# Loads and stores of a 1-D max pooling kernel, issued from GpSimd as one packet per DMA engine

## The chip, the cores and the metric

The kernel runs on one core of a Trainium2 chip. A core has five instruction queues: TensorE, VectorE, ScalarE, GpSimd and SyncE (SP); all but the first matter here. Its 16 DMA engines move data between the chip's memory (DRAM) and the on-chip buffer of 128 partitions. The metric is the device time of one execution in microseconds, the median of several runs. The profile is one further execution.

## What is computed

The input is float32 with 32 x 256 rows of 4096 values; the output has 256 values per row, each the largest of 16 neighbours.

```python
def reference(x: np.ndarray, output_size: int) -> np.ndarray:
    batch, channels, length = x.shape
    result = np.zeros((batch, channels, output_size), dtype=np.float32)
    for i in range(output_size):
        start = int(i * length / output_size)
        end = int((i + 1) * length / output_size)
        result[:, :, i] = np.max(x[:, :, start:end], axis=-1)
    return result
```

The input is 134.22 MB and the output 8.39 MB; 4096 / 256 = 16 without remainder, so every window has the same width W = 16.

## The kernel before

The 2,097,152 windows lie one behind the other in memory. They are dealt out in two groups, each cut evenly over the 128 partitions: group A has 9340 windows per partition, group B 7044. Within a group a partition's share is contiguous, so one row of a load is one contiguous stretch of memory.

**Loads.** Group A is read in ten loads (one of 128 windows per partition, eight of 1024, one of 1020), from the end of the share to its start; group B in seven (six of 1024, one of 900), from start to end. A load of 1024 windows is 128 rows of 65,536 bytes. The first, small one (line 87) goes to the space between the two slots' ends and serves to give VectorE work early; all others come from line 96.

**The ring.** The tile `ring` holds two slots of 1024 + 152 windows. A load uses one slot, and which 1024 of the 1176 windows it uses alternates: loads 0 and 1 lie at the low end of their slots, loads 2 and 3 are moved up by 152 (GAP), and so on. So the next load into a slot leaves 152 windows of the load before it untouched.

**Reductions.** `pooled` (line 56) is one VectorE reduction over the last axis. Each large load is reduced in two instructions: first the 872 windows that the next load into this slot will overwrite, then the 152 that it will not. The results go to the tile `kept` (the last load's to a part of the ring that has become free). The load after next can therefore be issued once the 872 are done, while the 152 are still being reduced.

**Stores.** Two large stores (line 117) write group A's and most of group B's results from `kept`. They stand behind all loads on SP's queue. The first needs nothing that is still to come when the last load has been issued; the second waits for the last reduction into `kept`. The last 900 windows per partition are stored by ScalarE (line 114), as soon as the last reduction ends.

**Order.** The framework derives the semaphores from the tiles. In the program, SP's queue holds the first load, two loads without waits, fourteen loads that each wait for a VectorE reduction (and for the landing of the load whose place they take), and the two stores. GpSimd's queue has four MEMSETs of constants at the start, which belong to the launch (line 134), and the barriers at the start and the end of the program. VectorE's queue holds only the reductions. All engines pass a barrier at the start and one at the end.

Of the kernel before, what the change touches and what calls it, by code (L numbers as in the profile page):

```python
# [1 line left out]

# [4 lines left out]


@with_exitstack
def kernel(  # L10
    ctx: ExitStack,
    tc: tile.TileContext,
    x: bass.AP,
    output_size: bass.AP,
    out: bass.AP,
):

    nc = tc.nc
    P = nc.NUM_PARTITIONS
    fp32 = mybir.dt.float32

    B, C, L = x.shape
    O = int(output_size)  # L30
    assert L % O == 0, (L, O)
    W = L // O
    total = B * C * O // P
    assert B * C * O % P == 0

    CHUNK = 1024
    GAP = 152
    FIRST = 128
    LOADS_A, LOADS_B = 9, 6

    LESS = 4
    group_a = [FIRST] + [CHUNK] * (LOADS_A - 1) + [CHUNK - LESS]
    last = total - sum(group_a) - LOADS_B * CHUNK
    group_b = [CHUNK] * LOADS_B + [last]
    assert 0 < last and last * (W + 1) <= CHUNK * W

    pool = ctx.enter_context(tc.tile_pool(name="pool", bufs=1))
    ring = pool.tile([P, 2 * (CHUNK + GAP) * W], fp32, tag="ring", name="ring")
    kept = pool.tile([P, total - last], fp32, tag="kept", name="kept")

    xw = x.flatten_outer_dims().rearrange("r (o w) -> (r o) w", w=W)
    ow = out.flatten_outer_dims().rearrange("r o -> (r o)")

    def pooled(dst, at, n):

        nc.vector.reduce_max(  # L56
            out=dst,
            in_=ring[:, at * W : (at + n) * W].rearrange("p (n w) -> p n w", w=W),
            axis=mybir.AxisListType.X,
        )  # L60

    taken = 0

    def group(n):

        nonlocal taken
        span = slice(taken * P, (taken + n) * P)
        taken += n
        return (
            xw[span].rearrange("(p n) w -> p (n w)", p=P),  # L70
            ow[span].rearrange("(p n) -> p n", p=P),
        )

    stores = []
    n_loads = 0
    base = 0
    for g, loads in enumerate((group_a, group_b)):
        xg, og = group(sum(loads))
        a = sum(loads) if g == 0 else 0
        for n in loads:  # L80
            if g == 0:
                a -= n
            xn = xg[:, a * W : (a + n) * W]
            dst = kept[:, base + a : base + a + n] if n != last else None
            if n == FIRST:

                nc.sync.dma_start(  # L87
                    out=ring[:, CHUNK * W : (CHUNK + n) * W], in_=xn
                )
                pooled(dst, CHUNK, n)  # L90
            else:

                low = n_loads % 2 * (CHUNK + GAP)
                moved = n_loads // 2 % 2
                at = low + moved * GAP
                nc.sync.dma_start(out=ring[:, at * W : (at + n) * W], in_=xn)
                if n != last:
                    cut = CHUNK - GAP if moved else GAP
                    parts = [(0, cut), (cut, n)]
                    for u, v in parts if moved else parts[::-1]:  # L100
                        pooled(dst[:, u:v], at + u, v - u)
                else:
                    end = (at + CHUNK) * W
                    last_kept = ring[:, end - n : end]
                    pooled(last_kept, at, n)
                n_loads += 1
            if g:
                a += n
        full = a - last if g else sum(loads)
        stores.append((og[:, 0:full], kept[:, base : base + full]))  # L110
        base += full
    assert taken == total

    nc.scalar.dma_start(out=og[:, full : full + last], in_=last_kept)
    tc.no_sync_barrier()
    for dst, src in stores:
        nc.sync.dma_start(out=dst, in_=src)


# [1 line left out]
_INS = ['x', 'output_size']  # L121
_OUTS = [((32, 256, 256), 'float32')]

_NUMBERS = {'output_size': 256}


# [26 lines left out]
```

## Time and profile before

| | |
|---|---|
| median of 3 runs | 334.98 us (334.91 to 335.12) |
| profiled execution's own span | 333.1 us |
| large loads: number, KB each, us from issue to landing (median) | 14 of the same size at 24.0 us; 8160 KB at 23.9; 7200 KB at 21.7 |
| first load | 1024 KB, 4.7 us |
| stores from SP | 4670 KB, 32.4 us; 3072 KB, 18.2 us |
| store from ScalarE | 450 KB, 4.2 us |
| reduction of 872 windows | 14 times, mean 14,686 ns |
| reduction of 152 windows | 15 times, mean 2,676 ns |
| reduction of the last 900 | 15,143 ns |
| length of a DMA instruction on SP's queue | 327 to 426 ns |
| memory read / written | 134.22 MB / 8.39 MB, 428 GB/s over the span |

The times of runs are taken without the profiler and include what lies around the profiled span. "Issue to landing" runs from the DMA instruction on its queue to the semaphore that says that all its data are there; a transfer that is queued behind another one has the other's remaining time in it. In the views by window the columns are: the stretch and its length, busy time of VectorE and of GpSimd with the number of instructions, the clock granted to TensorE (not used here), the mean share of time in which the 16 DMA engines had a packet, and the rate. A packet is booked whole where its record falls, so shares over 1 and rates that jump appear in stretches shorter than the packets of the loads; only longer stretches, or stretches with short packets, can be read as shares. Transfers are listed by queue: q1 is SP's, q10 is ScalarE's.

### The profile page before, as it was taken

The page shows a single profiled execution, that of the slowest core. Times are in us where ns is not written, and L with a number is a line of the kernel's source. Part 1 is how long each engine was busy: PE and PEld are TensorE (multiplying, and loading weights), DVE is VectorE, ACT ScalarE, POOL GpSimd, SP SyncE. Part 2 cuts the span into 40 slices and gives each one's busy share as a digit, 9 for nine tenths or more (in the row PEclk, how much of TensorE's full clock was granted, in tenths as well). Part 3 has the DMA queues.
Part 4 walks back from the last instruction along what each step waited for, and adds up shares of the span by engine and source line. Part 5 has one row for each costly group of instructions (what it writes and reads, how often), then busy time and mean ns, then how long its engine had stood idle before and what let it go on. Part 6 is the DMA issues. An engine that isn't in the chain of part 4 may idle for free.

```text
span 333.1 us, 113 instructions
## 1 busy us (share of the span) xinstructions
DVE 276.5 (83%) x32; POOL 0.2 (0%) x4
## 2 busy tenths in 40 slices
DVE  2009979797997979799797979979797998979993
POOL 0000000000000000000000000000000000000000
DMA  9898989899898989899898989899898989899997
GB/s 378 378 504 378 504 378 504 378 449 433 378 504 378 504 378 504 378 441 441 384 494 377 504 378 504 378 456 425 386 496 378 504 378 504 378 458 443 393 395 330
DMA packets 2880, 142.61 MB, mean 428 GB/s; under 512 B 320, under 2 KB 320, under 8 KB 448
## 3 DMA queue, kind: packets, MB, share of 16 engines
q1 hardware_dynamic: 2736, 142.15, 98.8%
q10 hardware_dynamic: 144, 0.46, 0.3%
HBM read 134.22 MB, written 8.39 MB: 428 GB/s over the span
## 4 chain that ended last, share of the span: by engine, by line
DMA 57%; DVE 36%; DVEq 5%; issue 0%; SPq 0%
DMA ring<-in_x_dram 57%; DVE kept L56 36%; DVEq L148 5%; SPq L87 0%
## 5 line engine op out<-in xcount | busy, mean ns | idle before, releaser
L56 DVE TENSOR_REDUCE kept<-ring 128x152 f32<-128x2432 f32 (+3 forms) x31 | 261.4, 8473 | 51.5 <-DMA ring<-in_x_dram 51.5
L56 DVE TENSOR_REDUCE ring<-ring 128x900 f32<-128x14400 f32 x1 | 15.1, 15143 | 0.0
L134 POOL MEMSET const-bfloat16-1.0<- 128x1 bf16 x1 | 0.1, 103 | 0.0
L134 POOL MEMSET const-uint8-127<- 128x1 uint8 x1 | 0.1, 102 | 0.0
L134 POOL MEMSET const-float32-0.0<- 128x1 f32 x1 | 0.1, 100 | 0.2 <-issue 0.2
L134 POOL MEMSET const-float32-1.0<- 128x1 f32 x1 | 0.1, 99 | 0.0
## 6 DMA issues: line engine op xcount, KB each, us to landing
ring<-in_x_dram SPq DMA_DIRECT2D x1, 8160.0 KB, 23.9
ring<-in_x_dram SPq DMA_DIRECT2D x1, 7200.0 KB, 21.7
out_dram<-kept SPq DMA_DIRECT2D x1, 4670.0 KB, 32.4
out_dram<-kept SPq DMA_DIRECT2D x1, 3072.0 KB, 18.2
ring<-in_x_dram SPq DMA_DIRECT2D x1, 1024.0 KB, 4.7
out_dram<-ring ACTq DMA_DIRECT2D x1, 450.0 KB, 4.2
ring<-in_x_dram SPq DMA_DIRECT2D x14, 24.0
```

The source lines that it names most:

```text
L56: nc.vector.reduce_max(out=dst, in_=ring[:, at * W : (at + n) * W].rearrange("p (n w) -> p n w", w=W), axis=mybir.AxisListType.X,)
L134: nc = _bacc.Bacc("TRN2", target_bir_lowering=False, num_devices=1)
L148: with _tile.TileContext(nc) as tc:
```

## The change

In three places `nc.sync.dma_start` becomes `nc.gpsimd.dma_start` with `single_packet=True`: the first load, the other sixteen loads, and the two large stores. Sizes, addresses, order and the waits of the transfers stay as they are: GpSimd's queue now has the nineteen DMA instructions between the start's and the end's barrier, and SP's has none. The flag asks that all that one DMA engine moves for one transfer is put into one packet. ScalarE's store stays as it is. The reductions are the same instructions in the same order, and wait for the same transfers.

```diff
@@ -84,8 +84,8 @@
             dst = kept[:, base + a : base + a + n] if n != last else None
             if n == FIRST:
 
-                nc.sync.dma_start(
-                    out=ring[:, CHUNK * W : (CHUNK + n) * W], in_=xn
+                nc.gpsimd.dma_start(
+                    out=ring[:, CHUNK * W : (CHUNK + n) * W], in_=xn, single_packet=True
                 )
                 pooled(dst, CHUNK, n)
             else:
@@ -93,7 +93,9 @@
                 low = n_loads % 2 * (CHUNK + GAP)
                 moved = n_loads // 2 % 2
                 at = low + moved * GAP
-                nc.sync.dma_start(out=ring[:, at * W : (at + n) * W], in_=xn)
+                nc.gpsimd.dma_start(
+                    out=ring[:, at * W : (at + n) * W], in_=xn, single_packet=True
+                )
                 if n != last:
                     cut = CHUNK - GAP if moved else GAP
                     parts = [(0, cut), (cut, n)]
@@ -114,7 +116,7 @@
     nc.scalar.dma_start(out=og[:, full : full + last], in_=last_kept)
     tc.no_sync_barrier()
     for dst, src in stores:
-        nc.sync.dma_start(out=dst, in_=src)
+        nc.gpsimd.dma_start(out=dst, in_=src, single_packet=True)
```

## The prediction

> **What bounds the kernel now.** I read the page's slices, queues and chain first, then the timeline of VectorE, then the waits of SyncE's queue, then narrow windows at the two ends.
>
> ```profile
> span 333.1 us, 113 instructions
> DVE 276.5 (83%) x32; POOL 0.2 (0%) x4
> DMA packets 2880, 142.61 MB, mean 428 GB/s; under 512 B 320, under 2 KB 320, under 8 KB 448
> q1 hardware_dynamic: 2736, 142.15, 98.8%
> q10 hardware_dynamic: 144, 0.46, 0.3%
> DMA 57%; DVE 36%; DVEq 5%; issue 0%; SPq 0%
> ```
>
> The 16 DMA engines are busy 98.8% + 0.3% of the span; VectorE 83%, GpSimd nothing. The chain's "DVE 36%" misleads: it follows buffer releases, but the engines carry on with the load before while VectorE frees a slot. Packets are 144 per transfer (2736 / 144 = 19 transfers on q1): 9 per engine, eight data rows and one that only signals (20 x 16 = 320 under 512 B).
>
> ```profile
> 44.13 17.28 DVE L56 TENSOR_REDUCE kept<-ring 128x872 f32<-128x13952 f32 x2 [2.07 <-DMA ring<-in_x_dram]
> 63.48 17.28 DVE L56 TENSOR_REDUCE kept<-ring 128x872 f32<-128x13952 f32 x2 [2.07 <-DMA ring<-in_x_dram]
> ```
> ```profile
> 24.78 14.70 DVE kept L56
> 39.48 0.02 issue
> 39.49 23.96 DMA ring<-in_x_dram
> 63.45 0.02 issue
> ```
>
> The first column is the start, the second the length. Loads land 63.48 - 44.13 = 19.35 us apart: 8,388,608 B / 19.35 us = 433.5 GB/s, 27.09 per engine. Each load is issued when the large reduction of the load two before it ends (39.49), 44.13 - 39.49 = 4.64 us before the load ahead has landed. So the queue never runs dry: I call 4.64 us the lead. VectorE idles 2.07 us per load.
>
> ```profile
> SPq L96 <- DVE kept L56: 205.5, 14, 14.7
> SPq L96 <- DMA ring<-in_x_dram: 78.4, 14, 22.7
> SPq L117 <- DVE kept L56: 21.1, 1, 21.1
> ```
>
> Fourteen loads wait so; the second store waits for the last reduction into kept.
>
> ```profile
> 1.40:1.60 0.20, 0.00 (x0) 0.00 (x0) 1.00 0.00 0
> 1.60:1.80 0.20, 0.00 (x0) 0.00 (x0) 1.00 1.63 287
> 2.20:2.40 0.20, 0.00 (x0) 0.00 (x0) 1.00 0.20 41
> 331.40:331.60 0.20, 0.00 (x0) 0.00 (x0) 1.00 0.52 198
> 331.60:331.80 0.20, 0.00 (x0) 0.00 (x0) 1.00 0.01 0
> ```
>
> The last two columns are the DMA share and GB/s. Packets run from 1.6 to 331.6 us. The span is therefore 1.6 us of start, 330.0 us of transfer and 1.5 us of end, and only these three can move.
>
> **The change, part by part.** Nineteen DMA instructions (17 loads, 2 stores) leave SP and go, in the same order with the same waits, to GpSimd, whose queue otherwise has four MEMSETs and the barriers. ScalarE's store stays. SP is left with nothing. The waits on VectorE move with the DMAs: behind a waiting load on GpSimd stand only later loads and the stores, as on SP, so nobody new waits.
>
> *Start.* SP issues the first load at 0.73 us and its first packet runs at 1.6, so 0.87 us from issue to packet. The trace has no DMA from GpSimd. Low end: GpSimd's last MEMSET ends at 0.33 + 0.10 = 0.43 us, 0.30 before SP issues, so -0.3 us if its path is otherwise equal. High end: the first load takes 4.7 us to land, of which 1,048,576 B / 433.5 GB/s = 2.4 are transfer; if the other 2.3 came twice, +2.3 us. I take one more 0.87, +0.9 us, since the nearest row is SP's own issue and I let GpSimd pay it twice. Nothing lies ahead to hide it. The following two loads are covered by the 2.4 us of the first. The Trainium skill (DMA: Bandwidth & Descriptors, Latency and other measured facts) speaks against the move: the first byte comes after about 0.6 us from SP and about 1 us from GpSimd. By that page this term would be an estimated +0.4 us, and the whole sum 0.5 us lower; its 0.6 stands against 0.87 here.
>
> *Middle, issue.* Fourteen loads would each have their packets later by the same 0.9 us. The cover is the lead: 4.64 us, of which SP's own path uses 0.87, so 3.77 us are free. Price 0; there is no gain to be had either, since no packet waits there. With the high end of 2.3 us later it is still 0. If the cover goes, the excess is paid 14 times, 14 us for each microsecond of excess. The skill warns that descriptors written by GpSimd starve while VectorE holds a shared port, but says that tensor_reduce on trn2 never takes it (SBUF — State Buffer, Who interferes with whom); no run here shows either, and by its rule this price stays 0.
>
> *Middle, packets.* One packet per engine removes eight packet borders per transfer. What is a border worth? The small store on q10 in the last stretch (from 324 us to the end) shows it:
>
> ```profile
> q10 hardware_dynamic: 144, 0.46, 12.7%
> out_dram<-ring ACTq DMA_DIRECT2D x1, 450.0 KB, 4.2
> ```
>
> 12.7% of 16 engines x 9.1 us is 18.5 us; 460,800 B at 27.09 GB/s is 17.0 us; 1.5 us / 144 is 10 ns per packet. Nineteen transfers x 8 borders x 10 ns = 1.5 us: the low end is -1.5. The high end is 0, since the 16 signal packets alone can be the 1.5 us (94 ns each) and they remain. I take -0.4, nearer to nothing, because the long packets of the loads leave no gap to close (share 1.01):
>
> ```profile
> 44.80:47.20 2.40, 2.40 (x1) 0.00 (x0) 1.00 1.01 437
> ```
>
> The skill (DMA: Bandwidth & Descriptors, Why small descriptors are slow) gives about 3 cycles per packet and calls packing worthwhile only at 256 B or less. By it the term would be an estimated 152 x 3 cycles at 850 MHz, or -0.5 us; the 10 ns here are an upper bound of what it says.
>
> *Middle, rate.* The bytes and the 16 engines are the same. I take 0. The high end comes from the slowest busy row for long packets, the stretch of the first store:
>
> ```profile
> DMA packets 144, 4.58 MB, mean 424 GB/s; under 512 B 16, under 2 KB 16, under 8 KB 16
> ```
>
> 424 against 433.5 is 2%, over some 310 us of loads +6.8 us. A gain beyond the packet term I exclude: the engines are already at full share.
>
> *End.* The second store and ScalarE's store share the engines from 328 us:
>
> ```profile
> 328.00:329.00 1.00, 0.00 (x0) 0.00 (x0) 1.00 0.92 393
> ```
>
> If an engine finishes a packet before it turns to another queue, which no row shows, ScalarE's small store must now wait for the second store's one packet of 196,608 B instead of slipping in between its rows. The bytes are the same: store two ends 460,800 B / 433.5 GB/s = 1.1 us sooner, and the small store follows. Low end -0.25 (the share of 0.92 over the three microseconds from 328 closes), high end +0.6 (its packets of 3.6 KB alone lose what the 8 KB packets lost from 1.6 to 2.6 us: 0.16 MB moved, worth 0.38 us, in 1.0 us). I take +0.2. The closing 0.9 us, from the landing at 327.99 + 4.2 = 332.2 to 333.1, now has GpSimd with 19 finished DMAs in its final barrier: low end 0, as nothing of this is shortened; high end the same again, +0.9. I take +0.3, nearer to nothing, since no work is added by the instructions.
>
> Sum: +0.9 + 0 - 0.4 + 0 + 0.2 + 0.3 = +1.0 us, on the profiled execution's 333.1: 334.1. The median of the runs is 334.98, 1.9 above that span, and lies around the span in both kernels: 336.0 us.
>
> **The rivals.**
>
> *One packet pays, the start does not* (the other side: faster). One mechanism: borders inside a transfer cost the full 10 ns and vanish. -1.5 for packets, the start at +0.3, midway between its low end and my value, the end at 0: 334.98 - 1.2 = 333.8. It decides as soon as the packet saving exceeds start plus end by 0.7 us. For it: the 10 ns. Against it: the share of 1.01, which leaves no visible gap. Chance 0.20.
>
> *Everything is hidden.* GpSimd starts 0.3 us before SP could and uses it up, borders give some tenths, ends cancel: 335.0. For it: lead and full queue, so that 330 of 333 us cannot notice who issues. Against it: the first load has no cover. Chance 0.21.
>
> *The queue runs dry or slow.* If GpSimd needs more than 4.64 us from released wait to first packet, each further microsecond costs 14; at 5.0 us it is 14 x 0.36 = +5.0, plus 5.0 - 0.87 = +4.1 at the start, 344.1. If instead engines lose 1% of their rate, +3.3 us plus the 1.0: 339.3. For it: GpSimd's preparation of a transfer's 144 rows and signals is nowhere in the trace. Against: it has 19.35 us per load and 3.77 of slack. Chance 0.12.
>
> *The change doesn't do what it says*: the transfers stay at nine packets per engine. Then the packet term is 0 and the sum +1.4: 336.4, inside the forecast's own range, and no case by itself.
>
> **How the numbers follow.** The forecast, slower by the start with nothing returned, has 0.47 and its own range 335.65 to 337.8 (+0.7 to +2.8: start near its value with no packet gain up to start +2.3 with +0.5 at the ends). No change can be told from the measurement within 0.2%, 0.67 us, here 334.31 to 335.65. Faster: the first rival, 0.20. Same: the second, 0.21. Slower: forecast and third rival, 0.47 + 0.12 = 0.59. For 8 in 10 I leave out about 0.08 below 333.6, somewhat under the first rival's time, and about 0.12 above 338.3, the dry or slow queue.
>
> **What would show it.** The start: the first non-empty DMA window moves from 1.6 to about 2.5 us, and the first reduction from 5.44 to about 6.3. The lead: reductions still 19.35 us apart and VectorE idle 2.07 before each; a larger spacing proves the third rival, a spacing under 19.30 the first. The packets: the count of 2736 falls to 19 x 16 = 304 if a record is a packet; if a record is a row, it stays. The end: ScalarE's store lands after the second store, later than 4.2 us from issue. I am wrong if the spacing moves by more than 0.05 us, since 16 loads turn that into 0.8 us, as much as the start.

## The result, and the profile after

The changed kernel takes 336.34 us (median of 4 runs, 336.10 to 336.95) against 335.05 us of the kernel before, run beside it (4 runs, 334.91 to 335.23): a ratio of 1.0043, with a 95% interval of 1.0029 to 1.0057. That is 1.3 us slower. The profiled execution has a span of 334.6 us, 1.5 us more than before.

The page of the changed kernel, in the order in which the page of before was read:

```profile
span 334.6 us, 114 instructions
DVE 276.5 (83%) x32; POOL 10.4 (3%) x23
DMA packets 2880, 142.61 MB, mean 426 GB/s; under 512 B 320, under 2 KB 320, under 8 KB 448
q0 software_dynamic: 2736, 142.15, 98.4%
L96 POOL DMA_DIRECT2D ring<-in_x_dram x16 | 8.4, 528 | 283.0 <-DVE kept L56 283.0
```

VectorE's work is the same to the tenth of a microsecond. GpSimd's nineteen DMA instructions now count as busy time and make 10.2 of its 10.4 us, so it is far from being a bound. All transfers of SP's q1 are now on a queue q0 of another kind, with the same 2736 records: nothing in the count says that nine packets have become one. If a record is a row, the count could not show it either; the runs below can.

The timeline at the start and in the loop (start, length, engine, what; in brackets the idle time before and what ended it):

```profile
1.26 0.67 POOL L87 DMA_DIRECT2D ring<-in_x_dram  x1 [0.82 <-PEq L150]
1.93 1.05 POOL L96 DMA_DIRECT2D ring<-in_x_dram  x2
6.30 2.29 DVE L56 TENSOR_REDUCE kept<-ring 128x128 f32<-128x2048 f32 x1 [6.30 <-DMA ring<-in_x_dram]
25.66 17.28 DVE L56 TENSOR_REDUCE kept<-ring 128x872 f32<-128x13952 f32 x2 [17.07 <-DMA ring<-in_x_dram]
40.64 0.53 POOL L96 DMA_DIRECT2D ring<-in_x_dram  x1 [37.66 <-DVE kept L56]
45.01 17.28 DVE L56 TENSOR_REDUCE kept<-ring 128x872 f32<-128x13952 f32 x2 [2.07 <-DMA ring<-in_x_dram]
83.79 17.28 DVE L56 TENSOR_REDUCE kept<-ring 128x872 f32<-128x13952 f32 x2 [2.05 <-DMA ring<-in_x_dram]
103.71 17.28 DVE L56 TENSOR_REDUCE kept<-ring 128x872 f32<-128x13952 f32 x2 [2.64 <-DMA ring<-in_x_dram]
297.27 17.28 DVE L56 TENSOR_REDUCE kept<-ring 128x872 f32<-128x13952 f32 x2 [2.18 <-DMA ring<-in_x_dram]
314.46 15.14 DVE L56 TENSOR_REDUCE ring<-ring 128x900 f32<-128x14400 f32 x1
329.64 0.37 ACTq L116 DMA_DIRECT2D out_dram<-ring  x1
```

The last two reductions in the timeline of the kernel before:

```profile
295.62 17.28 DVE L56 TENSOR_REDUCE kept<-ring 128x872 f32<-128x13952 f32 x2 [2.07 <-DMA ring<-in_x_dram]
312.82 15.14 DVE L56 TENSOR_REDUCE ring<-ring 128x900 f32<-128x14400 f32 x1
```

The first load is issued at 1.26 us (before: 0.73), the first large load is reduced from 25.66 (before: 24.78): 0.88 us later. A second profile of the kernel before, shown below, has 24.98, so this figure is good to some 0.2 us. From there most loads are 19.35 us apart as before (45.01 - 25.66), so the loop is not slower as such. Single loads are: 103.71 - 83.79 = 19.92, and two others 19.46. From the first large load to the last, 297.27 - 25.66 = 271.61 us, against 295.62 - 24.78 = 270.84 before: 0.77 us more. From the last reduction to the end of the span it is 334.6 - 314.46 = 20.14 us, against 20.28. So 0.88 + 0.77 - 0.14 = 1.5 us, the whole difference of the spans: a later start, a few long spacings, and no loss at the end.

Narrow windows of the start (length, busy time of VectorE and GpSimd, clock, DMA share, GB/s), the first two of the kernel before and the last two of the changed one:

```profile
1.65:1.70 0.05, 0.00 (x0) 0.00 (x0) 1.00 0.00 0
1.70:1.75 0.05, 0.00 (x0) 0.00 (x0) 1.00 0.42 164
2.60:2.65 0.05, 0.00 (x0) 0.05 (x1) 1.00 0.00 0
2.65:2.70 0.05, 0.00 (x0) 0.05 (x1) 1.00 2.63 492
```

Packets begin at 2.65 us instead of 1.70, 0.95 us later (in windows of 0.2 us, 2.6 instead of 1.6). Of this, 1.26 - 0.73 = 0.53 us is a later issue and (2.65 - 1.26) - (1.70 - 0.73) = 0.42 us a longer way from issue to packet. The Trainium skill (DMA: Bandwidth & Descriptors, Latency and other measured facts) has 0.4 us between the first bytes of the two paths; the second part agrees with it, and the page says nothing of the first part. Most of the first part is time in which GpSimd waits for nothing that the profile shows. In the chain of the changed kernel that is the first line here (the barrier is passed at 0.84 us); the second is the same gap in the loop, between the end of a reduction and the DMA instruction that waited for it:

```profile
0.84 0.42 issue
40.35 0.28 issue
```

In the chain of the kernel before, SP has 0.07 us at the start (from 0.67) and 0.02 us in the loop (at 39.48).

### The profile page after: what moved, and what is told of

Same layout as the page of the kernel before. It is cut to its first block, busy times and chain, and to the rows that moved or that the text cites. A ratio compares the mean times of both kernels' runs of the same rounds, so it can differ in the third digit from the quotient of the medians.

```text
span 334.6 us, 114 instructions
## 1 busy us (share of the span) xinstructions
DVE 276.5 (83%) x32; POOL 10.4 (3%) x23
## 3 DMA queue, kind: packets, MB, share of 16 engines
q0 software_dynamic: 2736, 142.15, 98.4%
## 4 chain that ended last, share of the span: by engine, by line
DMA 57%; DVE 36%; DVEq 5%; issue 1%; POOL 0%; PEldq 0%
DMA ring<-in_x_dram 57%; DVE kept L56 36%; DVEq L150 5%; POOL ring L87 0%; PEldq L150 0%
## 5 line engine op out<-in xcount | busy, mean ns | idle before, releaser
L96 POOL DMA_DIRECT2D ring<-in_x_dram x16 | 8.4, 528 | 283.0 <-DVE kept L56 283.0
L119 POOL DMA_DIRECT2D out_dram<-kept x2 | 1.1, 536 | 21.0 <-DVE kept L56 21.0
L87 POOL DMA_DIRECT2D ring<-in_x_dram x1 | 0.7, 667 | 0.8 <-PEq L150 0.8
## 6 DMA issues: line engine op xcount, KB each, us to landing
out_dram<-kept POOLq DMA_DIRECT2D x1, 3072.0 KB, 17.8
```

The source lines that it names most:

```text
L87: nc.gpsimd.dma_start(out=ring[:, CHUNK * W : (CHUNK + n) * W], in_=xn, single_packet=True)
L96: nc.gpsimd.dma_start(out=ring[:, at * W : (at + n) * W], in_=xn, single_packet=True)
L119: nc.gpsimd.dma_start(out=dst, in_=src, single_packet=True)
```

## The experiments

Each time is a median. Each ratio, with its 95% interval in brackets, goes against the kernel before, measured on the same chip beside it (335.02, 334.93 or 334.96 us).

**The engine alone, the flag alone.** All from GpSimd without the flag, and all from SP with it:

```diff
-nc.gpsimd.dma_start(out=..., in_=..., single_packet=True)
+nc.gpsimd.dma_start(out=..., in_=...)                      # first kernel
+nc.sync.dma_start(out=..., in_=..., single_packet=True)    # second kernel
```

> All nineteen transfers from GpSimd, without the one-packet flag. Main theory (a later start of 0.9 us and one DMA engine that falls behind by some 0.7 us; the flag does nothing): 336.3 us as with the flag, first reduction at 6.3 us, at least one spacing of two loads above 19.6 us. Rival 1 (the flag's long packets make the engine fall behind): start alone, 335.9 us, all spacings 19.35. Rival 2 (the flag returns 0.4 us of packet borders, as predicted): 336.7 us and spacings a little over 19.35.

> All nineteen transfers from SP as before, with the one-packet flag. Main theory: 335.0 us, nothing moves. Rival 1 (the flag makes an engine fall behind): 335.7 us with the start unmoved at 5.44. Rival 2 (the flag returns 0.4 us or more): 334.6 us or less, spacings under 19.33. If the count of packets, the lengths and the time all stay as before, SP may ignore the flag, and this run says nothing of it.

Measured: 336.34 us from GpSimd without the flag, 1.0038 [1.0026, 1.0051], the same as with it, and with a long spacing too (19.86 us); 334.99 us from SP with the flag, 1.0001 [0.9993, 1.0010], the same as before. The loss comes with the engine, and none that can be told with the flag. On SP alone the run would not tell whether the flag is heeded; on GpSimd later runs do.

One thing went against the main theory. The kernel from SP with the flag shows a long spacing as well, in its timeline:

```profile
82.90 17.28 DVE L56 TENSOR_REDUCE kept<-ring 128x872 f32<-128x13952 f32 x2 [2.05 <-DMA ring<-in_x_dram]
102.62 17.28 DVE L56 TENSOR_REDUCE kept<-ring 128x872 f32<-128x13952 f32 x2 [2.43 <-DMA ring<-in_x_dram]
```

19.72 us, without any transfer from GpSimd. So long spacings are not GpSimd's alone.

**The start alone.** The first load back on SP, the rest as in the changed kernel:

```diff
-nc.gpsimd.dma_start(
-    out=ring[:, CHUNK * W : (CHUNK + n) * W], in_=xn, single_packet=True
-)
+nc.sync.dma_start(
+    out=ring[:, CHUNK * W : (CHUNK + n) * W], in_=xn
+)
```

> The first load of 1 MB from SP without the flag, the other eighteen transfers from GpSimd with it. Main theory: the first load's 2.4 us of transfer cover GpSimd's later start, first reduction back at 5.44 and the first 872 windows at 24.8; what stays is the engine that falls behind, 335.6 to 335.7 us. Rival (the start is all of it): 335.0 us. Rival (the start has no part, the loss lies in the middle and at the end): 336.3 us.

Measured: 335.35 us, 1.0009 [1.0000, 1.0018]. The timeline:

```profile
0.74 0.37 SPq L87 DMA_DIRECT2D ring<-in_x_dram  x1
1.27 1.20 POOL L96 DMA_DIRECT2D ring<-in_x_dram  x2 [0.82 <-PEq L150]
5.27 2.29 DVE L56 TENSOR_REDUCE kept<-ring 128x128 f32<-128x2048 f32 x1 [5.27 <-DMA ring<-in_x_dram]
24.93 17.28 DVE L56 TENSOR_REDUCE kept<-ring 128x872 f32<-128x13952 f32 x2 [17.37 <-DMA ring<-in_x_dram]
```

GpSimd still issues at 1.27, but SP's 1 MB is on its way and covers it: the first large load is reduced from 24.93 us, which lies between the 24.78 and 24.98 of the two profiles of the kernel before. That returns 336.34 - 335.35 = 1.0 of the 1.3 us. The time fell below the 335.6 that the main theory gave. The profile fits that: from the first to the last large load it has 271.17 us, 0.33 more than before and not 0.77.

**Is it the chip?** The kernel before, profiled again:

> The kernel before, unchanged, profiled once more beside the others. It shows whether a long spacing of two loads (19.6 to 19.9 us once or twice in a run) also comes without GpSimd. Theory that GpSimd's transfers make an engine fall behind: all spacings 19.35 to 19.38. Rival (it comes with the chip or the moment, and is no part of the change): a spacing above 19.6 here too. Time 335.0 us in both.

334.96 us. All spacings lie between 19.29 and 19.36, and from 24.98 to 295.82 it is 270.84 us, exactly as in the first profile of before. From the last reduction to the end it is 333.2 - 313.01 = 20.19 us. This run settles less than it set out to: it was on another chip than the three runs above, and a long spacing came from SP with the flag. Each of the two chips has profiles with long spacings and profiles without.

**Only the first load from GpSimd,** with and without the flag:

```diff
-nc.sync.dma_start(
-    out=ring[:, CHUNK * W : (CHUNK + n) * W], in_=xn
-)
+nc.gpsimd.dma_start(
+    out=ring[:, CHUNK * W : (CHUNK + n) * W], in_=xn, single_packet=True   # and once without the flag
+)
```

> Only the first load from GpSimd with the flag, the other eighteen transfers from SP. Main theory: SP's second transfer is issued at about 0.8 us, ahead of GpSimd's first, so the engines start at 1.6 us on large rows; the order of the two is swapped or shared, the DMA engines are busy from 1.6 us and the end is within 0.3 us of before, 334.8 to 335.3 us, with the first reduction later than 6.3 us. Rival (whatever goes through GpSimd costs its own time at the start): 335.9 us.

> Only the first load from GpSimd, as in the run of that name, but without the flag. If the flag made one packet of the transfer, its 8 rows per engine would have gone out together, and without it the transfer should be later than 27.6 us or take turns where it did not before. If the flag changes nothing here: 337.6 us, first reduction at 27.6 us, 16 records of each queue in 3 us, as with it.

Measured: 337.65 us, 1.0077 [1.0064, 1.0091], with the flag, and 338.25 us, 1.0095 [1.0081, 1.0108], without. I had expected no loss, since the engines have SP's large loads to do from 1.7 us on. They did, but the order cost it. The timeline with the flag:

```profile
0.74 0.86 SPq L96 DMA_DIRECT2D ring<-in_x_dram  x2
1.23 0.65 POOL L87 DMA_DIRECT2D ring<-in_x_dram  x1 [0.78 <-PEq L148]
27.58 36.66 DVE L56 TENSOR_REDUCE kept<-ring 128x128 f32<-128x2048 f32 x5 [27.58 <-DMA ring<-in_x_dram]
```

VectorE's first instruction needs the 1 MB load and waits for it until 27.58 us, with a large load long there behind it. The next load waits for VectorE and is issued at 44.49 us. By then the engines have finished the first three loads. The first line is that issue, the second sums up all records from 42.7 to 45.2 us:

```profile
44.49 17.51 SPq L96 DMA_DIRECT2D ring<-in_x_dram  x2
DMA packets 16, 0.00 MB, mean 0 GB/s; under 512 B 16, under 2 KB 16, under 8 KB 16
```

No row starts there; the only records are the sixteen signals of the third load, which come between 43.4 and 44.1 us. The next rows start at 45.4 us, so the engines stand still for 1.4 to 2 us each. The rest of the 2.7 us was lost before: 17.8 MB at 433.5 GB/s would have been done at 1.7 + 41.1 = 42.8 us. The transfers by queue from 14 to 17 us show why the small load is so late:

```profile
DMA packets 32, 1.18 MB, mean 393 GB/s; under 512 B 0, under 2 KB 0, under 8 KB 0
q1 hardware_dynamic: 16, 1.05, 80.6%
q0 software_dynamic: 16, 0.13, 10.3%
```

In 3 us each queue has 16 records, as many as there are DMA engines, and so it goes on in the windows of 3 us before and behind. So an engine evidently takes one row of 64 KB from SP's queue, then one of 8 KB from GpSimd's, in turn, although this load has the flag. Without the flag the same window has the same lines. The nine records that each engine has of this load (eight rows and a signal) are thus spread over nine turns, and 393 GB/s is all that the turns move. The flag does not make a unit of the transfer.

**The end alone, tried twice.** The stores from GpSimd; then the stores and the last load:

```diff
-        nc.sync.dma_start(out=dst, in_=src)
+        nc.gpsimd.dma_start(out=dst, in_=src, single_packet=True)
...
-                nc.sync.dma_start(out=ring[:, at * W : (at + n) * W], in_=xn)  # second kernel only
+                eng = nc.gpsimd if n == last else nc.sync                      # second kernel only
+                eng.dma_start(out=ring[:, at * W : (at + n) * W], in_=xn)      # second kernel only
```

> Only the two large stores from GpSimd with the flag, all loads from SP. Main theory (the end costs nothing that can be measured): 334.9 to 335.2 us. Rival (the stores and the final barrier of GpSimd hold the 0.3 us that remain when the first load is on SP): 335.3 us or more.

> The last load and the two large stores from GpSimd, all else from SP, so that the first store stands behind the last load as before. It prices the end alone. Main theory (start 1.0, middle about 0.3, end nothing): 334.9 to 335.2 us. Rival (the end holds the 0.3 us): 335.3 us. As the prediction put it (the end costs 0.5): 335.5 us.

Measured: 345.29 us, 1.0314 [1.0295, 1.0334], for the stores alone, the largest loss of all runs that change only who issues, and a miss of every theory. The timeline of that kernel:

```profile
197.18 0.67 POOL L117 DMA_DIRECT2D out_dram<-kept  x1 [196.73 <-DVE kept L56]
199.21 17.28 DVE L56 TENSOR_REDUCE kept<-ring 128x872 f32<-128x13952 f32 x2 [2.34 <-DMA ring<-in_x_dram]
231.25 17.28 DVE L56 TENSOR_REDUCE kept<-ring 128x872 f32<-128x13952 f32 x2 [14.76 <-DMA ring<-in_x_dram]
325.97 15.14 DVE L56 TENSOR_REDUCE ring<-ring 128x900 f32<-128x14400 f32 x1
```

and its windows at the end:

```profile
336.00:338.00 2.00, 2.00 (x1) 0.00 (x0) 1.00 0.00 0
338.00:340.00 2.00, 2.00 (x1) 0.00 (x0) 1.00 0.00 0
340.00:342.00 2.00, 1.12 (x1) 0.00 (x0) 1.00 0.00 0
```

On a queue of its own the first store has only its data to wait for, and goes at 197.18 us, when group A is reduced, instead of after the last load. It delays the loads by 12.7 us (231.25 - 199.21 is 32.0 instead of 19.35 us), and is then missing at the end, where it used to keep the engines busy under the last reductions: the engines stand still for some 7 us, from the end of the second store at 335.0 to ScalarE's at 342. The bytes are the same. In the changed kernel this doesn't happen because loads and stores move together and keep their order.

With the last load also moved, 335.50 us, 1.0014 [1.0005, 1.0023], the very figure that the prediction's price of the end gave, but not by what it named: the last load now takes turns with the load before it, whose landing slips from 295.62 to 297.79. SP's queue in that kernel from 294.7 to 295.4 us and from 295.4 to 297.5:

```profile
q1 hardware_dynamic: 15, 0.00, 1.2%
q1 hardware_dynamic: 1, 0.00, 0.0%
```

Fifteen signals of the load before are there, and the sixteenth, a record without data, comes some 2 us later, behind a row of GpSimd's load. From the last reduction on this kernel takes 333.7 - 314.98 = 18.7 us, less than before. So the run does not price the end cleanly either. The end is priced by the traces alone: 20.14 us from the last reduction on, against 20.28 and 20.19 in the two profiles of the kernel before.

**GpSimd's issue without cover.** The lead is taken away in both kernels, once from SP and once from GpSimd; 96 windows of each large load are reduced twice:

```diff
-    GAP = 152
+    GAP = 8
...
-    ring = pool.tile([P, 2 * (CHUNK + GAP) * W], fp32, tag="ring", name="ring")
+    ring = pool.tile([P, (2 * (CHUNK + GAP) + FIRST) * W], fp32, tag="ring", name="ring")
+    home = 2 * (CHUNK + GAP)
...
-out=ring[:, CHUNK * W : (CHUNK + n) * W]
+out=ring[:, home * W : (home + n) * W]
...
+                    pooled(dst[:, 16:112], at + 16, 96)
```

> From SP, with the lead taken away: GAP is 8 instead of 152, the first load has a place of its own, and VectorE reduces 96 windows of each large load twice, so that it is done about 19 us after a load has landed. The next load is then issued when the engines have run dry. Estimated from 19.05 us of reductions, 0.9 from release to packet, 0.45 from last byte to reduction, against 19.3 of transfer: 1.1 us too late; if every load but the first ones pays half of it (two loads are under way at a time) 14 x 0.55 = 7.7, 343 us; if each pays all, 350 us.

> The same kernel with all loads and the large stores from GpSimd with the flag. It measures what GpSimd's issue costs inside the loop once nothing covers it. Main theory: GpSimd is 0.73 us later from release to packet (0.26 until it issues, 0.47 until the first packet), and as the delay is shared by two loads, 14 x 0.37 = 5.1 more, and 1.0 at the start: 6 us over the same kernel from SP. As the prediction put it (the excess is paid 14 times in full): 10.2 + 1.0 = 11 us over it. Rival (only the first issue is slow): 1.0 to 1.3 us over it.

Measured: 355.05 us from SP, 1.0600 [1.0577, 1.0622], and 359.44 us from GpSimd, 1.0723 [1.0702, 1.0744]. The first is 12 us above the 343 of my estimate and 5 above its 350: a queue that has run dry cost far more here than the issue and the last byte that I had added up, and what the rest is stays open. The mean spacing over 13 loads is (314.66 - 44.04) / 13 = 20.82 us, 1.47 over 19.35. The second is 4.4 us over the first. Less the 1.0 of the start that is 3.4 us, or 0.24 us per waiting load; in the two profiles it is 0.10 us (a mean spacing of 20.92 against 20.82). Both are under the 0.37 of the main theory, and far from the full 0.73 that the prediction's rule would charge 14 times. The four runs of each kernel lie 2 us apart, so neither figure is sharp.

The traces show how long the way is. The third large load waits for the reductions of the first; these, and the windows in which the third load's rows begin, from SP and then from GpSimd:

```profile
24.70 18.94 DVE L56 TENSOR_REDUCE kept<-ring 128x96 f32<-128x1536 f32 x3 [17.07 <-DMA ring<-in_x_dram]
44.40:44.60 0.20, 0.20 (x1) 0.00 (x0) 1.00 0.00 0
44.60:44.80 0.20, 0.20 (x1) 0.00 (x0) 1.00 11.03 3604
25.57 18.94 DVE L56 TENSOR_REDUCE kept<-ring 128x96 f32<-128x1536 f32 x3 [17.05 <-DMA ring<-in_x_dram]
45.80:46.00 0.20, 0.20 (x1) 0.00 (x0) 1.00 0.00 0
46.00:46.20 0.20, 0.20 (x1) 0.00 (x0) 1.00 9.23 2949
```

From the end of the reductions (43.64 and 44.51 us) to the first rows it is 1.0 us from SP and 1.5 us from GpSimd. So the issue inside the loop costs 0.5 us more than SP's, about half of it before the DMA instruction and half behind it, and not the 0.73 that my estimate had; at the start it is 0.95. Half of 0.5, shared by two loads as the main theory has it, would be the 0.24 of the medians, but the 0.10 of the profiles is less, and how the delay spreads over the loads stays open.

**What a piece costs.** From GpSimd, the rows of the large loads cut into pieces of 16 KB, without and with the flag:

```diff
-in_=xn
+in_=xn, max_dma_last_dim=16384
```

> All from GpSimd without the flag, the rows of the large loads cut into pieces of 16 KB: 33 packets per engine instead of 9 and so 24 more borders in 16 loads. If a border or a piece costs 10 ns, as the prediction's bound has it: 16 x 24 x 10 ns = 3.8 us, 340.2 us and spacings of 19.6. If it costs next to nothing: 336.3 us and 19.35.

> The same with the flag. If the flag takes away borders that cost 10 ns: 336.2 us against 340.2. If the cost belongs to the piece, or the flag does nothing here: as without the flag, within 0.3 us.

Measured: 339.20 and 339.15 us, both 1.0125. The queue's line on the page of the kernel without the flag (records, MB, share):

```profile
q0 software_dynamic: 8880, 142.15, 98.9%
```

and two of its loads in the timeline:

```profile
45.53 17.28 DVE L56 TENSOR_REDUCE kept<-ring 128x872 f32<-128x13952 f32 x2 [2.29 <-DMA ring<-in_x_dram]
65.11 17.28 DVE L56 TENSOR_REDUCE kept<-ring 128x872 f32<-128x13952 f32 x2 [2.30 <-DMA ring<-in_x_dram]
```

19.58 us between loads, 0.23 more, for 24 more pieces per engine: 0.23 / 24 = 9.5 ns per piece. The 10 ns that the prediction read from ScalarE's small store is right in size. But the flag takes none of it away: with the flag the spacing is the same 19.58 and the count 8880. The times are 1 us under the 340.2 that this price gave, which fits the 0.77 us of long spacings in the kernel without pieces: with pieces there are none.

## Why the prediction was right

The forecast was 336.0 us and the measured time is 336.34, inside the range and on the forecast side.

*Start, +0.9.* Right in sum: packets 0.95 us later, the first reduction 0.86, and 1.0 us comes back when SP issues the first load. The parts were wrong, so that the sum fits is partly luck. I let GpSimd issue when SP does and pay 0.87 us more from issue to packet. In fact it issues 0.53 us later than SP, and pays 0.42 more. SP's own way was misread too, from a window of 0.2 us: its first packets run at 1.70 us, not 1.6, 0.97 us after the issue. The low end, GpSimd ready at once after its MEMSETs, was far off: its first DMA starts 0.8 us after them.

*Middle, issue, 0.* Right. Issue at 40.64, landing of the load ahead at 45.01: 4.37 us of lead are left and GpSimd needs 1.4 from issue to packet at the start, and 1.2 in the loop of the kernel without lead. VectorE does not hold it up: its DMA instructions take 0.53 us in the loop, right beside running reductions, as long as each of the two at the start (1.05 us), when VectorE has nothing to do, and that agrees with the Trainium skill's rule that tensor_reduce leaves GpSimd's port free (SBUF — State Buffer, Who interferes with whom). The rule that an excess is paid fourteen times in full was not supported: with the lead gone the loss per load (0.24 or 0.10 us) was half of the 0.5 us that GpSimd's way to the first packet is longer, or less.

*Middle, packets, -0.4.* Wrong: 0. The size of a border, 10 ns, was right. What failed is that the flag would remove borders: from GpSimd each engine still has nine records per transfer, takes them singly in turn with another queue's, and is no faster for the flag. What a transfer would cost that really is one packet per engine, no run shows. The fourth rival, that the change doesn't do what it says, was true of the packets, and its 336.4 us is the nearest of all the figures given.

*Middle, rate, 0.* The undisturbed spacing is the same 19.35 us. But long spacings came on top: 0.77 us in the profile of the changed kernel, and the same 0.77 without the flag. They were not foreseen. Spread over the 14 spacings that is 0.055 us, just past the 0.05 us that the prediction named as the sign of being wrong.

*End, +0.5.* Wrong: the profiles show nothing, 20.14 us against 20.28 and 20.19. ScalarE's store lands 4.2 us after its issue as before, and the nineteen finished DMAs cost GpSimd's last barrier nothing.

So the sum +1.0 was near +1.3 because the packets' 0.4 of gain and the end's 0.5 of loss, both absent, nearly cancel, which is luck, and the long spacings, which it did not have, made up the rest. In the runs: 1.0 us of start is shown by putting the first load back; the remaining 0.3 us (interval 0.0 to 0.6) fits the long spacings, but no run separates them.

## What to carry to other kernels

Where every wait of the loop had microseconds of queued transfers behind it, who issues cost nothing here; so look at the first transfer, which nothing covers, and leave that one on the queue that starts earlier. Before transfers are moved to another queue, list what their old queue's order was doing: stores that move away from behind the loads cost about ten times here what the issuing engine did (10.4 us against 1.0). And a per-packet price read from a trace says nothing of which flag removes it.

## What was not expected of the hardware

The long spacings. Single loads land 0.1 to 0.6 us late, and the lag is not made up afterwards. The main theory put it down to one of the 16 DMA engines falling behind. The views add the engines up, but each load ends with sixteen signals, one per engine, and these decide it. All records of the kernel with only its first load from GpSimd and no flag, from 123.4 to 124.1 us and from 124.1 to 124.6 us, at the end of a load that comes 19.56 us after the one before:

```profile
DMA packets 30, 0.98 MB, mean 1404 GB/s; under 512 B 15, under 2 KB 15, under 8 KB 15
DMA packets 2, 0.07 MB, mean 131 GB/s; under 512 B 1, under 2 KB 1, under 8 KB 1
```

Fifteen signals (under 512 B) come in time, 19.3 to 19.4 us after those of the load before, and one alone is late. A short pause of all engines would have moved all sixteen. It is not always one: at the longest spacing of the changed kernel, 19.92 us, the first signal comes 19.47 us after the first of the load before and the last 19.94, so all are a little late and the last most of all.

In the profiles the first to the last large load took 270.84 us twice in the kernel before, 271.36 from SP with the flag, 271.17 with GpSimd after the first load, and 271.61 twice with all from GpSimd. The kernel with only its first load from GpSimd and no flag, whose other loads are SP's, has three (19.49, 19.56 and 19.46), which is most of what it takes more than its twin with the flag. With 16 KB pieces there is none: the spacings are 19.57 to 19.59 (the load of 1020 windows aside), and the four runs lie within 0.07 us without the flag, where the four of the changed kernel spread over 0.85. What delays single engines, and whether GpSimd's queue makes it more frequent or these profiles are too few, stays open.
